# Emitting the steps of three recurrences behind every 24 products of a projection instead of every 12

## The chip, the cores and the metric

The kernel runs on one core of one Trainium2 chip. The metric is device time in microseconds (us); the kernel before took 1235.43 us, the median of three runs (1233.78 to 1237.32).

## What is computed

The reference is one layer of a hybrid model. 272 tokens (16 learned ones and 256 of the input, 2048 wide) are normalised and multiplied by one wide matrix. Its columns feed three mixers, each a recurrence over chunks of 64 tokens: A (`hgrn2`, 8 heads), B (`mlstm`, 4 heads) and C (`rwkv7`, 16 heads). Each result goes through a matrix and a gate, the three are added, and a last matrix and a norm follow:

```python
xn = rmsnorm(h, norm_g[l])
(a_q, a_f, ..., c_z, g_a, g_b, g_c) = split_cols(xn @ w_in[l])
y_a = hgrn2_mixer(a_q, a_f, a_i, a_z, ...)
y_b = mlstm_mixer(b_q, b_k, b_v, b_o, b_ig, b_fg, b_z, ...)
y_c = rwkv7_mixer(c_r, c_k, c_v, c_wd, c_ad, c_z, ...)
merged = (jax.nn.sigmoid(g_a) * (y_a @ w_br[l, 0])
          + jax.nn.sigmoid(g_b) * (y_b @ w_br[l, 1])
          + jax.nn.sigmoid(g_c) * (y_c @ w_br[l, 2]))
h = h + merged @ w_out[l]
return rmsnorm(h, final_norm_g)[:, N_META:]
```

## The kernel before, in words

**Precision and products.** Every weight and every activation is split into a high and a low half (`fp32r`), and a product of the reference becomes three matmuls: high by high, low by high, high by low. `unit` (line 379) does this for four row tiles of a weight block and one column tile: 12 matmuls.

**The weight stream.** `Stream` (from line 334) keeps four raw weight blocks of 128x1024 in flight (`load`, line 345, a transfer on SyncE's queue) and up to three split ones. `cut` (line 353) makes the halves: ScalarE copies the high one (`wh`), VectorE subtracts it for the low one (`wl`). Both happen inside `ws.next`, once for each block.

**The projections.** `gemm` (line 392) computes 256 columns for all tokens, transposed: four weight blocks, and in each of them two column tiles (`nt` is 2 for each call) of 12 matmuls into two PSUM banks of the tag `gp`, of which there are four. After the last block the banks are emptied (`evac`). The list `blocks` orders the projections: three of C's first group, the gates of B, then groups `b 0`, `c 1`, `b 1`, `c 2`, `a 0`, `a 1`, `c 3`, `a 2`, `a 3` (line 1591). A C group after the first is four calls of `gemm` (R, K, V, Z), an A group four (F, Q, I, Z), a B group eight. After these come the products of the gates and branches (`rows_gemm`, line 1358) and of the last matrix.

**The recurrences** are generators: `c_scan` (line 508), `b_scan` (967) and `a_scan` (1140). Each `yield` ends a step; `yield "pe"` says that the next step begins with a matmul. A C recurrence makes scores (`SC` from `RA` and `BK`), sends them through DRAM to a layout with 40 small matrices, inverts these in 31 steps on VectorE (`LV`, `Ltmp`, line 657), sends the result back (`scv`, `sct`, `Vm`, `VT`, lines 669 to 683), and then runs five chunks in order (line 733), each a chain of products and copies. It ends with a norm, with the bonus `cBV` added, in `Y["C"]` (lines 788 to 810). `cBV` uses the buffer of `cK`, which the next group's K projection writes.

**Who emits a step, and when.** `Order` (line 44) keeps a modelled clock for TensorE, ScalarE and VectorE while the program is written out. `pump` (line 87) goes through the open recurrences and emits steps as long as a step's modelled inputs are ready no later than 3.5 us after TensorE's clock; for a step that begins with a matmul the margin is 2.0 us for C and 0.3 us for A and B:

```python
ahead = self.AHEAD
if s["pe"]:
    ahead = self.AHEAD_PE if s["prio"] else self.AHEAD_PE_FIRST
if s["ready"] > self.clk["pe"] + ahead:
    break
self.step(s)
```

`finish` (line 105) emits all that is left of a recurrence. It is called where the next one needs its buffers: before C's next R projection (line 487), before the next head of B begins (950), before the next A recurrence begins (1124) and, up to the place where its tiles come free, before A's next F projection (1114). `pump` is called in `gemm` (line 399) and, after each three matmuls, in `rows_unit` (line 1356). The order in which the program is written out is a priority: the framework that builds it may place an instruction that it takes to be ready ahead of an earlier one that it takes to be waiting, unless `keep_in_program_order` is set (line 129).

Of the kernel before, what the change touches and what calls it, by code (L numbers as in the profile page):

```python
# [150 lines left out]
def kernel(  # L151
# [29 lines left out]
    od = Order()  # L181
# [197 lines left out]
    def unit(h, l, u, kts, ps, aH, aL, t0, n, js):  # L379
        for k in range(UK):  # L380
            kk = u * UK + k
            rh = aH[:, kk, t0:t0 + n]
            mm(ps, h[:, k, js], rh, start=kk == 0, stop=False)
            mm(ps, h[:, k, js], aL[:, kk, t0:t0 + n], start=False, stop=False)
            mm(ps, l[:, k, js], rh, start=False, stop=kk == kts - 1)

    def apart(f):
        saved, od.ready = od.ready, od.clk["pe"]
        f()
        od.ready = saved  # L390

    def gemm(m, aH, aL, kts, t0, n, evac):
        nt = m // P
        ps = [gps.tile([P, 512], F32, name="gp", tag="g") for _ in range(nt)]
        for u in range(kts // UK):
            h, l = ws.next()
            for j in range(nt):
                unit(h, l, u, kts, ps[j][:, 0:n], aH, aL, t0, n, slice(j * P, (j + 1) * P))
                od.pump()
        for j in range(nt):  # L400
            apart(lambda: evac(j, ps[j][:, 0:n]))

# [2 lines left out]
    def proj(c0, m, t0, evac, before=None, after=None):  # L405
        ws_src = win[:, :, c0:c0 + m]
        blocks.append((ws_src, KT, lambda: gemm(m, xH, xL, KT, t0, T - t0, evac), before, after))
# [1291 lines left out]
```

## Time and profile before

| what | before |
|---|---|
| median of 3 runs (lowest, highest) | 1235.43 us (1233.78, 1237.32) |
| the profiled execution's own time | 1238.05 us |
| its span, first to last instruction | 1236.3 us |
| TensorE matmuls busy | 1210.1 us |
| VectorE busy | 878.7 us |
| ScalarE busy | 665.7 us |

The profile is of one execution. PE is TensorE's matmul row, PEld its weight loads, DVE VectorE, ACT ScalarE, POOL GpSimd, and a q behind a name (SPq) is the engine's queue, which issues transfers. Times are counted from the first instruction. Matmuls are pipelined, so that a matmul shows as busy for some 0.28 us while the next starts 0.12 us after it. Nearly all instructions of VectorE and ScalarE carry line 127 and all matmuls line 186 (helpers), so tiles tell them apart: `gp` is a bank of a projection, `cbank` one of the C recurrence, `bank` one of A or B.

### The profile page before, as it was taken

To read this page: it belongs to the slowest core of one execution; us is meant where nothing else is said; L and a number is where in the kernel's file an instruction comes from. 1 tells how busy PE (TensorE), PEld (TensorE's weight loads), DVE (VectorE), ACT (ScalarE), POOL (GpSimd) and SP (SyncE) were. 2 spreads that over 40 slices of the span, in tenths; PEclk is the share of its full clock that TensorE was granted. 3 is DMA by queue.
4 is the path that set the end of the run, shared out by engine and by line. 5 is a ranking of instruction groups with operands and counts; after the bars stand their busy time and mean duration, and the time that the engine had idled before them with its cause. 6 is when DMAs were issued, how large, how long until landed. Compare 5 with 4: busy or idle time off the path is not lost.

```text
span 1236.3 us, 23074 instructions
## 1 busy us (share of the span) xinstructions
PE 1210.1 (98%) x9226; PEld 1106.3 (89%) x9226; DVE 878.7 (71%) x1489; ACT 665.7 (54%) x1032; POOL 57.2 (5%) x167
## 2 busy tenths in 40 slices
PE   7999999999999999999999999999999999999997
PEld 6999999999999999989999978888888888888887
DVE  5778897687985799995889986644555555556554
ACT  5764445564445764756764757544444444445444
POOL 3100000000041000000000000000000000000000
PEclk8999999999999999999999999999999999999999
DMA  8646555455563564554554454666766676665563
GB/s 211 186 142 175 159 156 137 137 168 157 157 178 103 154 163 139 154 154 116 150 169 130 139 164 135 205 189 191 231 191 193 198 219 198 196 190 171 193 196 120
DMA packets 173124, 207.43 MB, mean 168 GB/s; under 512 B 22395, under 2 KB 127224, under 8 KB 172632
## 3 DMA queue, kind: packets, MB, share of 16 engines
q1 hardware_dynamic: 172104, 202.73, 56.1%
q0 software_dynamic: 880, 3.22, 0.8%
q8 instruction: 72, 1.18, 0.4%
q14 instruction: 36, 0.29, 0.1%
q10 hardware_dynamic: 32, 0.01, 0.0%
HBM read 202.19 MB, written 3.74 MB: 167 GB/s over the span
## 4 chain that ended last, share of the span: by engine, by line
PE 84%; DVE 9%; ACT 3%; issue 2%; DMA 1%; SPq 0%; ACTq 0%; DVEq 0%
PE gp L186 76%; PE cbank L186 4%; DVE wl L127 3%; PE bank L186 3%; ACT wh L127 1%; DVE Ltmp L127 1%; DMA xt<-in_x_dram 1%; DVE LV L127 1%; PE cbank L193 1%; PE bank L193 1%; DVE UV L127 0%; DVE aM L127 0%; DVE aY L127 0%; ACT L127 0%; DVE aW L127 0%
## 5 line engine op out<-in xcount | busy, mean ns | idle before, releaser
L127 DVE TENSOR_TENSOR wl<-raw,wh 128x1024 fp32r<-128x1024 f32 (+1 forms) x370 | 449.1, 1215 | 242.2 <-ACT wh L127 240.7
L127 ACT CAST wh<-raw 128x1024 fp32r<-128x1024 f32 (+1 forms) x370 | 386.5, 1045 | 387.3 <-PE gp L186 358.2
L186 PE MATMUL gp<-xH,wh 128*128 128x272 f32 (+3 forms) x1552 | 449.5, 290 | 0.2 <-ACT xH L127 0.2
L186 PE MATMUL gp<-xH,wl 128*128 128x272 f32 (+3 forms) x1552 | 445.1, 287 | 1.6 <-DVE wl L127 1.6
L186 PE MATMUL gp<-xL,wh 128*128 128x272 f32 (+3 forms) x1552 | 444.8, 287 | 0.0
L186 PEld LDWEIGHTS gp<-xH,wl 128*128 128x128 f32 x1552 | 293.4, 189 | 3.0 <-DVE wl L127 2.7
L186 PEld LDWEIGHTS gp<-xH,wh 128*128 128x128 f32 x1552 | 293.7, 189 | 2.2 <-ACT xH L127 0.5
L186 PEld LDWEIGHTS gp<-xL,wh 128*128 128x128 f32 x1552 | 293.5, 189 | 0.8 <-DVE xL L127 0.2
L186 PE MATMUL gp<-wh,xH 128*128 128x512 f32 x384 | 150.7, 392 | 0.0
L186 PE MATMUL gp<-wh,xL 128*128 128x512 f32 x384 | 150.5, 392 | 0.0
L186 PE MATMUL gp<-wl,xH 128*128 128x512 f32 x384 | 150.2, 391 | 0.0
L186 PEld LDWEIGHTS gp<-wh,xL 128*128 128x128 f32 x384 | 72.1, 188 | 15.4
L186 PEld LDWEIGHTS gp<-wl,xH 128*128 128x128 f32 x384 | 72.2, 188 | 15.2
L186 PEld LDWEIGHTS gp<-wh,xH 128*128 128x128 f32 x384 | 72.1, 188 | 15.0
L186 PE MATMUL gp<-wh,mH 128*128 128x512 f32 (+1 forms) x144 | 51.1, 355 | 0.0
L186 PE MATMUL gp<-wl,mH 128*128 128x512 f32 (+1 forms) x144 | 51.0, 354 | 0.0
L186 PE MATMUL gp<-wh,mL 128*128 128x512 f32 (+1 forms) x144 | 50.9, 354 | 0.0
L127 DVE TENSOR_TENSOR LV<-LV,Ltmp 40x31 f32<-40x31 f32 (+15 forms) x124 | 41.0, 330 | 2.6
L127 DVE TENSOR_TENSOR Ltmp<-LU,LV 40x31 f32<-40x31 f32 (+15 forms) x124 | 41.0, 331 | 2.4
L186 PEld LDWEIGHTS gp<-wh,mL 128*128 128x128 f32 x144 | 27.2, 189 | 3.7
L186 PEld LDWEIGHTS gp<-wl,mH 128*128 128x128 f32 x144 | 27.2, 189 | 3.7
L186 PEld LDWEIGHTS gp<-wh,mH 128*128 128x128 f32 x144 | 27.2, 189 | 3.7
(412 smaller groups left out, 1476.5 us busy)
## 6 DMA issues: line engine op xcount, KB each, us to landing
raw<-in_w_in_dram SPq DMA_DIRECT2D x288, 512.0 KB, 3.6
raw<-in_w_br_dram SPq DMA_DIRECT2D x48, 512.0 KB, 3.8
raw<-in_w_out_dram SPq DMA_DIRECT2D x32, 512.0 KB, 3.6
hres<-in_x_dram POOLq DMA_DIRECT2D x2, 1024.0 KB, 5.8
raw<-in_w_in_dram SPq DMA_DIRECT2D x4, 256.0 KB, 2.9
fg<-in_final_norm_g_dram POOLq DMA_DIRECT2D x1, 1024.0 KB, 5.3
out_dram<-hres SPq DMA_DIRECT2D x4, 256.0 KB, 2.6
xt<-in_x_dram SPq DMA_DIRECT2D x3, 320.0 KB, 6.8
```

Source lines behind the costliest of these rows:

```text
L127: r = f(*a, **k)
L186: nc.tensor.matmul(o, lhsT, rhs, start=start, stop=stop)
L193: nc.tensor.transpose(o, a, i)
```

## The change

In `gemm` the call of `pump` moves out of the loop over the two column tiles. Steps of the recurrences are emitted after both tiles of a weight block, 24 matmuls, and no longer after each tile's 12.

```diff
@@ -396,7 +396,7 @@
             h, l = ws.next()
             for j in range(nt):
                 unit(h, l, u, kts, ps[j][:, 0:n], aH, aL, t0, n, slice(j * P, (j + 1) * P))
-                od.pump()
+            od.pump()
         for j in range(nt):
             apart(lambda: evac(j, ps[j][:, 0:n]))
```

## Rows read from the trace of the kernel before

**Rows 1.** The page: busy us (share of the span) xinstructions of each engine.

```profile
PE 1210.1 (98%) x9226; PEld 1106.3 (89%) x9226; DVE 878.7 (71%) x1489; ACT 665.7 (54%) x1032; POOL 57.2 (5%) x167
```

**Rows 2.** Busy time by stretch: length, each engine's busy us (xcount), clock, DMA.

```profile
core 0: us, PE busy (x) PEld busy (x) DVE busy (x) ACT busy (x) POOL busy (x), PEclk, DMA share, GB/s
40.00:771.00 731.00, 721.07 (x6891) 694.44 (x6891) 601.29 (x1177) 432.99 (x746) 45.09 (x131) 1.00 0.53 150
325.00:375.00 50.00, 50.00 (x457) 49.18 (x457) 42.88 (x85) 24.30 (x41) 16.22 (x62) 1.00 0.58 161
475.00:527.00 52.00, 50.42 (x577) 49.09 (x575) 50.44 (x117) 33.01 (x57) 0.32 (x2) 1.00 0.46 133
695.00:740.00 45.00, 41.97 (x537) 37.66 (x536) 40.81 (x93) 29.68 (x50) 1.01 (x2) 1.00 0.51 147
771.00:1128.00 357.00, 357.00 (x1574) 294.48 (x1573) 192.37 (x187) 160.02 (x170) 1.07 (x2) 1.00 0.66 200
```

**Rows 3.** Waits of TensorE's matmuls: for whom, us in total, times, longest us.

```profile
PE gp L186 <- DVE wl L127: 1.6, 4, 0.7
PE bank L186 <- DVE aW L127: 1.6, 2, 1.0
...
PE cbank L186 <- DVE SC L127: 1.5, 4, 0.6
PE cbank L186 <- issue: 1.4, 1, 1.4
PE bank L186 <- DVE aYL L127: 1.2, 2, 0.8
PE cbank L186 <- ACT cX L127: 0.9, 3, 0.3
```

**Rows 4.** Chain of waits, pumped stretch of 105 to 200 us: start, us, what.

```profile
128.48 1.41 PE gp L186 x12
...
130.33 4.26 PE gp L186 x36
...
141.14 5.64 PE gp L186 x48
...
154.56 10.69 PE gp L186 x84
```

**Rows 5.** Chain of waits, main loop of the first C recurrence.

```profile
217.96 1.70 PE gp L186 x12
...
219.76 0.68 PE cbank L186 x4
220.44 0.75 PE gp L186 x6
221.19 0.63 PE cbank L186 x4
...
222.64 0.85 PE cbank L186 x24
```

**Rows 6.** Instructions by shape, the two halves: busy us, mean ns, idle before.

```profile
L127 DVE TENSOR_TENSOR wl<-raw,wh 128x1024 fp32r<-128x1024 f32 x366 | 446.4, 1221 | 242.2 <-ACT wh L127 240.7
L127 ACT CAST wh<-raw 128x1024 fp32r<-128x1024 f32 x366 | 384.1, 1050 | 387.3 <-PE gp L186 358.2 <-issue 22.4 <-ACT osq L127 1.6
```

**Rows 7.** Timeline, end of the second C recurrence: start, us, instruction [idle before].

```profile
415.36 0.69 DVE L127 TENSOR_TENSOR cYc<-cYc,cBV 128x512 f32<-128x512 f32 x1
...
416.08 0.87 ACT L127 ACTIVATE cK<-gp,omu 128x272 f32<-128x272 f32 x2 [0.53 <-DVE cYc L127]
...
416.51 0.39 PE L186 MATMUL gp<-xH,wh 128*128 128x256 f32 x1
```

**Rows 8.** Timeline of SyncE's queue, second C recurrence.

```profile
356.28 0.39 SPq L669 DMA_DIRECT2D scv<-LV  x1
359.44 0.38 SPq L350 DMA_DIRECT2D raw<-in_w_in_dram  x1
359.87 0.42 SPq L197 DMA_DIRECT2D sct<-LT  x1
```

## The prediction

> **What bounds the kernel now.** I began with the page's engine totals [rows 1]: TensorE is busy 1210.1 us of the 1236.3 us span, VectorE 878.7. The table by stage came next [rows 2]. In it the reader should subtract the busy column of PE from the length of each stretch. Over the 731 us in which recurrences run, 9.9 us are left over; in the 357 us of gate and branch products none. Where the A and C recurrences crowd VectorE (50.44 of 52 us, 40.81 of 45 us) TensorE loses 1.58 and 3.03 us. Its granted clock is 1.00, the upper level of 2.4 GHz, in every row. So the projections bound the kernel, and the recurrences cost time only where a product of theirs, or a late weight half, makes TensorE wait.
>
> Then I asked who ends those waits [rows 3]. From 40 us on they are: the low weight half 1.6 us, `aW` 1.6, `SC` 1.5, one product 1.4 (listed as issue), `aYL` 1.2, `cX` 0.9; the rest are below 0.6 each. This list is the whole store that a different grain could empty.
>
> Last I read the chain of waits for how recurrence products sit among projection products. In a pumped stretch [rows 4] runs of `gp` products are 12, 36, 48 or 84 long: 12 last 1.41 us, and a run that is an odd multiple of 12 shows groups standing in the middle of a weight block. From 44 to 771 us I counted about 42 such mid-block positions in this view against some 30 at block ends. In the main loop of a C recurrence [rows 5] the runs are 6 and 12 and the groups come every 1.43 to 1.45 us: this part is emitted by `finish` when the next group opens (line 487), and the build then places each product by its own idea of readiness. That half of the work never sees the removed call.
>
> **The change, part by part.** No instruction is added or removed. Of about 376 pump calls in `gemm` every second one goes (47 calls of `gemm`, 4 blocks, 2 tiles); the pumps in `rows_unit`, every 3 products, stay.
>
> *What the steps are moved past.* Between the two pump places of a block the program emits 12 matmuls and nothing else. Loads are issued and halves cut only in `ws.next`, evacuations only after the last block. So on VectorE, ScalarE, GpSimd and SyncE a step moved from mid-block to block end passes nothing: its order against the split (1.05 us on ScalarE, 1.22 us on VectorE, [rows 6]) and against the weight load is the old one. Only on TensorE is it moved, behind 12 products: 1.41 us. Cost of the non-TensorE steps: 0. What covers it is that the test `ready <= pe + 3.5` at the block's end admits what the two tests admitted together; were that cover gone, a split would stand behind other steps than now, and its 1.22 us on VectorE could come late once in a block.
>
> *Products that were early.* A product placed 1.41 us later finds its input there. Both `aYL` waits (longest 0.8 us) are shorter than 1.41, and by my count of products from the start of the group both stand mid-block. I take 1.2 us off. The `aW` and `SC` waits stand partly at block ends or in steps forced by `finish`: bounds 0 and 3.1 us off; I take 0, since `SC` waits for a PSUM bank that VectorE empties just as late. The `aW` inputs hang on the same crowded VectorE.
>
> *Products that were just in time.* A chain of recurrence steps that passes through TensorE slips 1.41 us, or a whole block of 2.82 when it misses the next test. The tightest consumer I found is the handover after the second C group [rows 7]: `cYc` waits for the bonus `cBV` until 416.05, `cK` is evacuated at 416.08 (0.53 us idle for it), and the next projection's first product runs at 416.51. There is no slack. ScalarE and VectorE are in order there, so a late `cYc` holds both evacuations and, behind them, the bank that the product needs. I price it at one slip: +1.4 us. Bounds: 0, since two more banks may come free first, and 2.82.
>
> *A and B.* Their products have a margin of only 0.3 us and so slip by 1.41 or 2.82 us at a step rather than clump. Their results are needed by the branch products, hundreds of us later, and the first tile that the next head overwrites is one projection away (8 x 1.41 = 11.3 us). Cost 0; without that slack, 2.82 for the one head.
>
> *A step that slips a whole block* does pass one split and one load. For the transfers of a C recurrence that matters on SyncE [rows 8]: `scv` went at 356.28, then a weight load held the queue, and `sct` followed at 359.87, 3.2 us after `scv` had been issued (356.28 + 0.39). A slip past one more load is bounded by 0 and 3.2 us; I take 0, as the old program already has a load in that place.
>
> *Sum.* -1.2 + 1.4 = +0.2 us. The profiled execution took 1238.05 us (span 1236.3 and 1.75 around it), 2.62 above the median of the three runs, 1235.43. Made against the profile the sum gives 1238.25; carried to the median, **1235.6 us**.
>
> **A rule against the change.** The rows show TensorE filling the links of a dependent chain with projection products: 6 of them, 0.75 us, between two groups 1.43 us apart [rows 5]. In the Trainium skill, "TensorE: Matmul & The Clock Gate", section "Step-by-step: what each phase is for", matmuls stay in program order and only weight loads are pulled ahead. By that rule two dependent groups put at the same block end, if the build leaves them adjacent, would leave the 0.75 us of such a link open; the row agrees in so far as the six products there do stand between the groups. This gives the second rival its mechanism; the row gives its price.
>
> **The rivals.** The first ends on the other side: **the C chain comes late**. Place: the handover of [rows 7] and its like after the first group. Three `RA,BK` groups and two transposes of `cV` precede the triangular inverse, and each may miss a test. Price: 2 handovers x 2.82 = 5.6 us, so 1241.0; with one transfer held behind a load, 3.2 more, 1244.2. It decides once the end of a C recurrence moves by more than the slack, which is nil after the second group. For it: VectorE is 42.88 of 50 us busy while the second inverse runs [rows 2], so little is made up. Against: the main loop is emitted by `finish` at a fixed place, which a small slip doesn't move, and the evacuation of `cV` doesn't need the recurrence.
>
> **Clumps**: two dependent groups at one block end. I found five pairs 12 to 15 products apart inside one block (four `RA,BK`, one of the decay products). Price: 5 x 0.75 = 3.8 us, 1239.2. For it: `SC` is already a wait. Against: in [rows 5] the build itself put 6 products between such groups.
>
> **Waits dissolve**: every pumped wait goes (`aYL` 1.2, `SC` 1.5, `aW` 1.6) and no chain is late: -4.3, so 1231.1. For it: 42 groups get 1.41 us more for their inputs. Against: `aW` and `SC` follow VectorE, which stays as full.
>
> **It does not do what it says**: the build orders products by readiness, as [rows 5] shows, and the new program order yields nearly the old stream. 1235.4.
>
> **How the numbers follow.** Differences under 0.3% (3.7 us) can't be told from no change here: the three runs spread over 1233.78 to 1237.32. My forecast has 0.45, the unchanged stream 0.10, both within 0.3%; the late C chain 0.15, clumps 0.10, both slower; dissolved waits 0.20, faster. That makes 0.20, 0.55, 0.25. Low end: 1231.1 less half the spread of the runs, 1.8, or 1229.3. High end: the late chain with a held transfer, 1244.2. The middle of all four rivals is inside; I leave two in ten for what I have not thought of.
>
> **What would show it.** Right: the same instruction counts; runs of `gp` products in pumped stretches that are multiples of 24; no TensorE wait for `aYL`; VectorE order around the splits as before; idle TensorE between 40 and 771 us still about 9.9 us. Late chain: the product after the second C group's handover starts after a gap, with `cK` evacuated later against it than now, and `LV` ending later. Clumps: more wait on `SC` and `cX`, and fewer `gp` products between groups. Dissolved: `aW` and `SC` leave the list. Wrong altogether: the low weight half rises in the list of waits, because then VectorE's order did change, or the C main loop is no longer emitted by `finish`.

## The result, and the profile after

The changed kernel takes 1248.28 us in the median of four runs (1246.7 to 1250.05), the kernel before 1234.71 (four runs, 1233.78 to 1237.32): a ratio of 1.0109, 95% interval 1.009 to 1.0128. It is slower by some 13.6 us. That lies outside the range I gave, on the side of the first rival, and in a place that I had not named.

The profiled run of the changed kernel took 1246.7 us (span 1245.0). First its page: TensorE's total, and of the slices the rows of TensorE, of its clock and of what the transfers moved.

```profile
PE 1212.8 (97%) x9226; PEld 1108.1 (89%) x9226; DVE 874.6 (70%) x1489; ACT 664.4 (53%) x1032; POOL 54.8 (4%) x167
...
PE   8999999999999999999999996999999999999997
...
PEclk8999999999999999999999997999999999999999
...
GB/s 216 195 128 195 151 154 151 119 170 149 167 174 114 153 173 143 128 189 110 148 174 130 154 162 28 214 187 189 231 189 195 192 212 211 191 195 174 189 198 120
```

The work is the same as in [rows 1]: 9226 matmuls, 1489 VectorE instructions. The reader should look for the one slice that stands out. It is the 25th (747 to 778 us): TensorE busy six tenths, its clock seven tenths of full, and 28 GB/s where its neighbours move 162 and 214. Something stopped the stream of weights for a whole slice.

The stretches of [rows 2], as far as they matter here, and below them a cut that [rows 2] did not make, at 700 us. Columns: length, each engine's busy us, granted clock, DMA share, GB/s.

```profile
40.00:771.00 731.00, 712.75 (x6839) 686.47 (x6838) 591.91 (x1171) 424.26 (x734) 42.32 (x130) 0.99 0.53 149
695.00:740.00 45.00, 42.49 (x443) 37.06 (x443) 43.82 (x97) 21.90 (x33) 0.00 (x0) 1.00 0.60 173
771.00:1128.00 357.00, 356.42 (x1562) 294.17 (x1563) 192.97 (x189) 160.02 (x172) 1.64 (x3) 1.00 0.66 197
```

```profile
40.00:700.00 660.00, 653.03 (x6182) 1.00 0.54 151
700.00:800.00 100.00, 88.14 (x780) 0.93 0.47 139
```

The same cut of the kernel before:

```profile
40.00:700.00 660.00, 653.10 (x6163) 1.00 0.54 151
700.00:800.00 100.00, 96.97 (x855) 1.00 0.53 159
```

This cut is the whole reading. Up to 700 us TensorE is idle 6.97 us after and 6.90 before: over nine tenths of the stretch with recurrences, and nearly all the waits I had weighed, come to no difference. From 700 to 800 us it is idle 11.86 us against 3.03. That is 8.8 us, and the clock of 0.93 comes on top.

TensorE's waits, over the whole profile (for whom, us in total, times, longest us), against [rows 3]:

```profile
PE cbank L186 <- ACT UV L127: 3.8, 6, 1.2
PE gp L186 <- DVE wl L127: 3.6, 4, 1.4
PE bank L193 <- ACT xt L127: 3.2, 1, 3.2
PE cbank L186 <- ACT cX L127: 3.2, 6, 0.7
PE cbank L186 <- DVE cSL L127: 2.9, 1, 2.9
PE bank L186 <- DVE aQ L127: 1.8, 2, 1.1
...
PE cbank L186 <- DVE UV L127: 1.4, 1, 1.4
PE cbank L186 <- DVE SC L127: 0.4, 1, 0.4
```

`aYL` has left the list, `SC` fell from 1.5 to 0.4 us, `aW` from 1.6 to 0.2: what the rival of dissolving waits said did happen. In their place stand `UV`, `cX` and `cSL`. `UV` and `cX` are links of a C recurrence's main loop, between whose groups six projection products stood in [rows 5]; `cSL` belongs to the norm behind the loop.

Which products ran there? The next view is that of the tile `gp`, the projections' accumulator, in the stretch 742 to 774 us of the changed kernel (duration ns min/median/max, first and last start):

```profile
L186 PE MATMUL gp<-wh,xL x1: 396/396/396, 743.1 to 743.1; 128*128 128x512 f32 x1
...
L186 PE MATMUL gp<-wh,yHB x2: 628/628/628, 772.6 to 773.4; 128*128 128x512 f32 x2
```

The last product of the first gate block (the first 96 products behind the projections) starts at 743.1 us, and the next projection product of any kind at 772.6: 29.5 us without one. The longest such stretch in the kernel before, from 700 us on, is 3.6 us. What TensorE did meanwhile, by stretches:

```profile
743.00:755.00 12.00, 10.25 (x114) 1.00 0.33 92
755.00:763.00 8.00, 4.51 (x62) 0.86 0.00 0
763.00:772.00 9.00, 3.78 (x26) 0.50 0.00 0
772.00:775.00 3.00, 3.00 (x11) 0.59 0.03 5
775.00:790.00 15.00, 15.00 (x67) 1.00 0.62 194
```

Left alone with the dependent steps of the fourth C recurrence, and for a while of an A recurrence, it is less and less busy, and no weights are loaded since none are used. The products that end the hole multiply `yHB`. Their casts, and the evacuation `sg` of the gate block that was finished at 743, come on ScalarE only when the recurrence writes its last chunk `cY`:

```profile
768.73 0.19 ACT L127 COPY cY<-cbank 128x32 f32<-128x32 f32 x1 [1.14 <-PE cbank L186]
768.95 0.60 ACT L127 ACTIVATE sg<-gp 128x512 f32<-128x512 f32 x1
...
771.09 1.12 ACT L127 CAST yHB<-yB 128x512 fp32r<-128x512 f32 x2
```

In the kernel's text `l_setup` (lines 1342 to 1345) lets the fourth C recurrence finish, closes its pool and opens the pool that holds `sg`, `yHB` and the merged sums. Whether these two wait for the memory or for their place in ScalarE's queue no run here tells apart.

Why then was the recurrence late? Two lines of the tiles `RA` and `BK`, 600 to 660 us, of the kernel before:

```profile
L186 PE MATMUL cbank<-RA,BK x40: 272/272/373, 633.6 to 640.7; 64*128 64x128 f32 x32, 64*128 64x32 f32 x8
...
L127 DVE TENSOR_TENSOR BK<-cK,cE x4: 178/432/690, 625.1 to 626.5; 64x512 f32<-64x512 f32 x2, 64x32 f32<-64x32 f32 x2
```

and of the changed one:

```profile
L186 PE MATMUL cbank<-RA,BK x40: 272/272/373, 646.4 to 655.0; 64*128 64x128 f32 x32, 64*128 64x32 f32 x8
...
L127 DVE TENSOR_TENSOR BK<-cK,cE x4: 176/424/689, 630.7 to 633.0; 64x512 f32<-64x512 f32 x2, 64x32 f32<-64x32 f32 x2
```

The first row's start, 633.6 and 646.4, moved by 12.8 us. The last operation on the data it multiplies starts at 626.5 and 633.0: the product came 7 us after its input before, and 13 us after it now. In the changed kernel `RA` was complete at 621.9 us, and TensorE has no idle time before the product (its busy time, clock, DMA share and GB/s):

```profile
633.00:646.30 13.30, 13.30 (x110) 1.00 0.60 164
```

So it was not waiting for data; it stood later in the order of TensorE's instructions. The main loop, whose first products are `cbank<-VT,SC`, then starts at 739.6 us instead of 723.6.

### The profile page after: what moved, and what is told of

It is laid out like the page before. It is cut to its first block, busy times and chain, and to the rows that moved or that the text cites. A ratio compares the mean times of both kernels' runs of the same rounds, so it can differ in the third digit from the quotient of the medians.

```text
span 1245.0 us, 23073 instructions
## 1 busy us (share of the span) xinstructions
PE 1212.8 (97%) x9226; PEld 1108.1 (89%) x9226; DVE 874.6 (70%) x1489; ACT 664.4 (53%) x1032; POOL 54.8 (4%) x167
## 4 chain that ended last, share of the span: by engine, by line
PE 86%; DVE 9%; ACT 3%; issue 1%; DMA 1%; SPq 0%; ACTq 0%; DVEq 0%
PE gp L186 77%; PE cbank L186 5%; PE bank L186 2%; DVE wl L127 2%; ACT wh L127 1%; DVE LV L127 1%; DVE Ltmp L127 1%; PE cbank L193 1%; DMA xt<-in_x_dram 1%; PE bank L193 1%; DVE aM L127 0%; DVE aW L127 0%; DVE aY L127 0%; DVE UV L127 0%; DVE aRS L127 0%
```

## The experiments

Two theories are told apart. **Late end**: a test of the planner lets out about one step of the C recurrence, so half the tests make it slow; only the fourth one is paid for, because the projections that can cover its end run out. **Spread**: the coarser grain makes steps wait for one another, a little in every block. The planner is plain arithmetic in the kernel, so one can count how many of the fourth recurrence's 94 steps are out when the group is flushed: 71 before, 55 after. The expectations use that count.

**1 and 2. Which part of the run.** A flag `od.fine` chooses the grain; `mark` is the first block of the fourth C group.

```diff
-                od.pump()
+                if j == nt - 1 or od.fine:
+                    od.pump()
...
+    for nb, (src, kts, run, before, after) in enumerate(blocks):
+        od.fine = nb >= mark
```

> Edit: tests behind whole blocks of 24 up to the projections of the fourth C group, behind each 12 from there on. Theory (late end): the 13.6 us are lost only because the fourth C recurrence, whose steps the planner admits about one per test, ends later, and the projections that could run beside its end have run out; the three earlier ones were 5 to 9 us late for nothing. With fine tests for the fourth the time comes back to 1235 to 1241 us (the planner has 64 of its 94 steps out when the group is flushed, against 71 in the kernel before and 55 in the changed one, so some of it may stay). Rival (lateness is handed on from group to group): 1246 to 1248 us. Rival (clumps, a loss at every block): the blocks from there on are about a third, so 1243 to 1245 us.

Measured: 1239.29 us, ratio 1.0044 (1.0029 to 1.0059). The second kernel has `nb < mark`:

> Edit: the reverse; tests behind each 12 products up to the projections of the fourth C group, behind whole blocks from there on. Theory (late end): most of the loss is here, 1242 to 1248 us (62 of 94 steps out at the flush). Rival (handed on): about 1235 us. Rival (clumps at every block): a third of 13.6 us, 1238 to 1240 us.

Measured: 1241.28 us, ratio 1.0061 (1.0046 to 1.0076). The first falls in the late end's range, the second 0.7 us below it. "Handed on" expected about 1247 and 1235 and is out, and the shares of a loss at every block, 1243 to 1245 and 1238 to 1240, are missed on either side. The main loop starts at 729.2 and 731.8 us, the stretch without projection products is 10.6 and 15.4 us. But the two losses, 5.6 and 7.5 us, are closer to each other than I thought: how the planner stands when the fourth group begins matters as well as what it does in it.

**3. The hole by itself.** The changed kernel, with the second gate block emitted before the first block of the branch product; the recurrences are not touched.

```diff
         for jb in range(D // WB):
             one(jb)
+        if first:
+            blocks.insert(n0 + 1, blocks.pop(n0 + 2))
```

> Edit: the changed kernel, with the second gate block of branch B emitted ahead of the first block of its output product, so that 96 more products of 512 columns that need nothing of the recurrences stand behind the first 96. The recurrences come as late as in the changed kernel. Theory (late end: TensorE stands idle because nothing independent is left from 743 to 772 us): these 96 products, some 20 us, run in the hole, and 8 to 13 of the 13.6 us come back: 1235 to 1240 us. Rival (the loss is spread, by clumps or by lateness in the stretch before): nothing comes back, 1247 to 1249 us.

Measured: 1232.28 us, ratio 0.9989 (0.9979 to 0.9998). All of the loss is gone, more than the 8 to 13 us expected. Its trace has the recurrence as late as in the changed kernel (`VT,SC` at 739.1 us) and the hole filled. Busy time by stretch, and what TensorE did from 752 us:

```profile
40.00:700.00 660.00, 652.94 (x6182) 1.00 0.51 151
700.00:800.00 100.00, 98.14 (x839) 1.00 0.53 167
```

```profile
752.32 0.68 PE L186 MATMUL cbank<-UV,SC 128*128 128x128 f32 x4
752.76 0.47 PE L186 MATMUL gp<-wh,xH 128*128 128x512 f32 x1
...
753.99 0.57 PE L186 MATMUL cbank<-cX,Vm 128*128 128x64 f32 x4
754.37 0.47 PE L186 MATMUL gp<-wh,xL 128*128 128x512 f32 x1
```

Idle time from 700 to 800 us is 1.86 us where the changed kernel had 11.86, and between `UV,SC` and `cX,Vm` stand gate products again. This is the run that decides: with the same tests at the same places, the grain costs nothing once there is something to run. Spread expected 1247 to 1249.

**4. Emission or data.** Tests at block ends, but each admits more.

```diff
-    AHEAD = 3.5
-    AHEAD_PE = 0.3
-    AHEAD_PE_FIRST = 2.0
-    CAP = 5.0
+    AHEAD = 4.9
+    AHEAD_PE = 1.7
+    AHEAD_PE_FIRST = 3.4
+    CAP = 6.4
```

> Edit: tests behind whole blocks as in the changed kernel, but the planner's three margins and its cap are 1.4 us larger (4.9, 1.7, 3.4 and 6.4 us), half a block of its own clock, so that a test admits the next step as well. Theory (late end, by one step per test): the fourth recurrence is as far at the flush as in the kernel before (75 of 94 steps against 71), 1233 to 1238 us. Rival (clumps: steps that stand 24 products apart wait for each other, whatever the margin): stays at 1246 to 1249 us, or above, as larger margins issue steps before their inputs are there.

Measured: 1236.46 us, ratio 1.0026 (1.0016 to 1.0037), within the late end's 1233 to 1238. `RA,BK` and `VT,SC` of the fourth recurrence start at 626.7 and 714.8 us, earlier than in the kernel before. The steps still stand 24 products apart, so their spacing was not the cost; when they were let out was. What is left, 2.7 us, has its place partly before 700 us, where TensorE is busy 1.2 us less (651.92 of 660).

**5. Place or number.** One test a block, behind its first 12 products.

```diff
-                od.pump()
+                if j == 0:
+                    od.pump()
```

> Edit: one test for each block of 24, as in the changed kernel, but behind its first 12 products instead of behind all 24. Theory (it is the number of tests that paces the fourth recurrence): 57 steps out at the flush against the changed kernel's 55, so 1244 to 1248 us. Rival (it is the place: behind a whole block the steps stand next to the next block's split, or wait 12 products longer than they need): 1234 to 1238 us.

Measured: 1247.44 us, ratio 1.011 (1.0096 to 1.0123); `VT,SC` at 738.3 us, 28.1 us without projection products. The place within the block is worth nothing: the number of tests is.

**6 and 7. Whose steps.** The mid-block test admits one kind of recurrence only (`pump` gets a filter for its scans).

```diff
-                od.pump()
+                od.pump() if j == nt - 1 else od.pump(lambda s: not s["prio"])
```

> Edit: the test at mid block admits steps of the C recurrence alone; A's and B's are admitted behind whole blocks. Theory (late end of the fourth C recurrence): C's own steps have both tests again, but A's, which share VectorE's modelled clock with them, come in larger doses; the planner has 65 steps of the fourth recurrence out at the flush (71 before, 55 changed), so 1236 to 1241 us. Rival (A's and B's coarser steps cost the time): 1246 to 1249 us. Rival (only the number of tests counts, whatever they admit): 1233 to 1235 us.

Measured: 1245.07 us, ratio 1.009 (1.0074 to 1.0106), a miss by 4 us and near the rival that blames A's and B's grain. With `s["prio"]` in place of `not s["prio"]`:

> Edit: the reverse; the test at mid block admits A's and B's steps alone, C's behind whole blocks. Theory (late end of the fourth C recurrence): the planner has 58 of its steps out at the flush, near the changed kernel's 55, so 1243 to 1248 us. Rival (A's and B's coarser steps cost the time): 1233 to 1237 us.

Measured: 1241.69 us, ratio 1.0061 (1.0047 to 1.0075), a miss by 1.3 us on the other side, and far above that rival's 1233 to 1237. So restoring the tests for C alone gives back little, and for A and B alone about half. In the planner both charge one modelled VectorE clock, so neither's steps come out independently of the other's. In the traces the fourth main loop starts at 737.6 and 734.0 us, late in both, in the order of the times; my count of steps at the flush (65 and 58) had them the wrong way round. In run 7 the fourth inverse starts 2.3 us earlier than in the kernel before (first `LV` update at 647.3 against 649.6 us) and its last update comes 11.9 us later (720.6 against 708.7): C's own 31 steps had half the tests. In run 6 it starts 7.3 us later and its last update comes 14.6 us later, though C had all its tests; what holds it up there is not shown. With C alone there is a second cost, busy 650.50 of 660 us before 700, and in TensorE's waits of that kernel (40 to 800 us) the low weight half has risen from 1.6 to 5.6 us:

```profile
PE gp L186 <- DVE wl L127: 5.6, 7, 1.6
```

**8. The hole in the kernel before.** The edit of run 3 on the fine tests.

> Edit: the kernel before (a test behind each 12 products), with the second gate block of branch B emitted ahead of the first block of its output product. Theory: in the kernel before, the products beside the end of the fourth recurrence last almost to its end, so little is left to fill: TensorE is idle 3.0 us between 700 and 785 us, and the change can give back that at most: 1230 to 1234 us. If it is no faster than the changed kernel with the same edit (1232.3 us), then with the hole filled the fineness of the tests costs and saves nothing that can be measured; the rival, that coarse tests also cost something in the stretch before, expects it 2 us or more below that one.

Measured: 1233.74 us, ratio 1.0002 (0.9993 to 1.0011): nothing to fill, nothing gained. Coarse with the hole filled (1232.28) is not slower than fine with it filled, which leaves nothing for a spread loss.

**9 and 10. Finer still.** In `unit`, a test after 6 of the 12 products as well; run 10 adds the two gate blocks.

```diff
             mm(ps, l[:, k, js], rh, start=False, stop=kk == kts - 1)
+            if k % 2 == 1 and k < UK - 1:
+                od.pump()
```

> Edit: the kernel before with four times the tests of the changed one, behind each 6 products (the order of the blocks as before). Theory (the number of tests paces the fourth recurrence, and only the hole at its end costs): the fourth recurrence ends some us earlier than in the kernel before, but there TensorE had only 3.0 us of idle time between 700 and 785 us, so 1231 to 1234 us. Rival (each finer dose is worth as much as the last): 24 to 12 products gave 13.6 us, 12 to 6 would give 5 to 7 us, 1227 to 1229 us. Rival (steps issued before their inputs are there, and TensorE waits for them in order): 1236 to 1242 us.

Measured: 1241.87 us, ratio 1.0065 (1.0042 to 1.0087).

> Edit: tests behind each 6 products and the second gate block of branch B emitted ahead of the first block of its output product. Theory: with the hole filled the fineness of the tests is worth nothing, so the time is that of the coarse kernel with two gate blocks (1232.3 us) within 2 us. Rival (fine tests also save waits before 700 us): 1228 to 1230 us.

Measured: 1243.93 us, ratio 1.0068 (1.005 to 1.0087). Both miss the theory and the expectation of a steady gain; the third reading, steps let out too early, has the size. There is no hole (3.1 us at most in either). The loss is before 700 us, as the stretches of run 9 show, and so the extra gate block can't help:

```profile
40.00:700.00 660.00, 649.97 (x6123) 1.00 0.54 150
700.00:800.00 100.00, 97.78 (x872) 1.00 0.54 161
```

Its waits name the low weight half and `SC`, against 1.6 and 1.5 us in [rows 3]:

```profile
PE gp L186 <- DVE wl L127: 4.1, 4, 1.4
PE cbank L186 <- DVE SC L127: 3.6, 5, 1.3
```

That is 4.6 us of the 7.8. Nor is the fourth recurrence earlier than at 12 products (`VT,SC` at 727.7 and 731.6 us against 723.6). The rest goes with TensorE's clock. Three of run 9's six executions had a mean granted clock of 0.996 and took 1237.7 to 1240.3 us; the other three, at 0.991 or 0.986, took 1243.4 to 1248.5. In run 10 two at 0.996 took 1238.3 and 1239.4 us, and four at 0.990 or 0.991 took 1243.5 to 1245.5. So at the higher clock the finer tests cost 3.6 to 6.2 us, and the 2 us between the two medians say nothing of the gate block; where the clock fell is shown at the end. So of these grains 12 products are best: at 6 weights and steps wait on VectorE, at 24 the last recurrence is late.

**11. Both cures at once**: the margins of run 4 and the gate blocks of run 3.

> Edit: the changed kernel with margins larger by 1.4 us and with the two gate blocks. Theory: the margins alone left 2.7 us over the kernel before although the fourth recurrence came 9 us earlier than there; that is put down to steps issued too early (1.2 us less TensorE work done from 40 to 700 us), which the gate blocks don't cure: 1233 to 1237 us. Rival (what is left there is the end of the recurrences too): 1230 to 1232 us.

Measured: 1236.53 us, ratio 1.002 (1.0011 to 1.0029). As expected: with the recurrence early there is no hole, and the 2.4 us that the margins cost stay.

**12. Run 3 again.**

> Edit: none against the run with the changed kernel and two gate blocks; it is taken again beside the others. Theory: 1231.5 to 1233 us, 0.1% below the kernel before, an interval that just leaves out 1. If it comes out within 0.05% of the kernel before, then no version here beats that one measurably.

Measured: 1233.75 us, ratio 0.9995 (0.9986 to 1.0003). The interval of the first run left out 1, this one does not, so the kernel with coarse tests and two gate blocks is as fast as the kernel before; that it is faster is not established.

The kernels side by side. "Bare" is the longest stretch from 700 us on, start to start, without a projection product; times in us. The medians of the kernel before that were taken beside the experiments are 1233.73 (1 to 4), 1233.75 (5 to 8) and 1234.1 (9 to 12).

| kernel | `VT,SC` of the fourth | bare | TensorE idle 40 to 700 | idle 700 to 800 | median |
|---|---|---|---|---|---|
| before | 723.6 | 3.6 | 6.9 | 3.0 | 1234.7 |
| changed | 739.6 | 29.5 | 7.0 | 11.9 | 1248.3 |
| 1, fine from the fourth group | 729.2 | 10.6 | 7.2 | 6.2 | 1239.3 |
| 2, coarse from the fourth group | 731.8 | 15.4 | 6.9 | 5.7 | 1241.3 |
| 3, changed, two gate blocks | 739.1 | 3.5 | 7.1 | 1.9 | 1232.3 |
| 4, larger margins | 714.8 | 3.3 | 8.1 | 1.6 | 1236.5 |
| 5, test at mid block only | 738.3 | 28.1 | 6.1 | 12.0 | 1247.4 |
| 6, C at mid block | 737.6 | 10.2 | 9.5 | 6.2 | 1245.1 |
| 7, A and B at mid block | 734.0 | 12.1 | 7.2 | 5.7 | 1241.7 |
| 8, before, two gate blocks | 720.9 | 2.8 | 7.0 | 1.6 | 1233.7 |
| 9, a test each 6 | 727.7 | 3.1 | 10.0 | 2.2 | 1241.9 |
| 10, a test each 6, two gate blocks | 731.6 | 3.1 | 9.9 | 2.2 | 1243.9 |
| 11, larger margins, two gate blocks | 714.6 | 3.3 | 8.0 | 1.6 | 1236.5 |
| 12, as 3 | 741.2 | 3.5 | 7.1 | 1.8 | 1233.8 |

## Why the prediction was wrong

**The step that failed** is the cover under the non-TensorE steps: "the test `ready <= pe + 3.5` at the block's end admits what the two tests admitted together". It does not. After a test the steps of A and the weight splits have charged the planner's VectorE clock up to the margin or past it, so the next step of C is priced to end beyond `pe + 3.5`, and the loop mostly stops after that one step. The planner's arithmetic for the fourth recurrence, carried through for both kernels (its own clock, us; steps counted from 0):

```
                 before                          changed
step   issued at pe   its end          issued at pe   its end
 13        700.7       705.4               739.8       743.8
 14        702.1       706.2               742.4       746.4
 15        703.4       708.2               745.2       749.1
 16        704.7       709.2               748.0       751.6
 23        715.7       720.7               763.2       768.1
```

In the changed column step 14 ends at 746.4 while the test stands at 742.4: 746.4 > 742.4 + 3.5, so the test ends there, and step 15 waits for the next one, 2.8 us on. In the column before, step 14 ends at 706.2 > 702.1 + 3.5 and the test ends as well, but the next is 1.3 us on. About one step per test in both, with half the tests: steps 13 to 23 take 15.0 us before and 23.4 after. I had treated the test as a gate on readiness, when on a crowded VectorE it is a metronome. The runs that show it: more margin at the same tests (run 4) brings the recurrence back, another place for as many tests (run 5) does not. The prediction had priced the loss of this cover at a split's 1.22 us, late once in a block; the waits for the low weight half rose by only 2.0 us in all (1.6 to 3.6), and the loss came at the end of the fourth recurrence instead, as 29.5 us without projection products and 8.8 us more idle time.

**The other points, in their order.**

- *Waits.* I took 1.2 us off for `aYL` and nothing for `aW` and `SC`; all three fell, by 1.2, 1.4 and 1.1 us. Others rose as much, and 40 to 700 us came out even (6.90 and 6.97 us idle).
- *The handover after the second C group* [rows 7], +1.4 us: it did not happen. From 405 to 425 us TensorE is busy 20.00 of 20.00 us, and so it was in the kernel before. I had read "no slack" from instructions that follow closely on one another; the rows show the bonus being added to `cYc` until 416.05, not a wait for it, and TensorE idle nowhere. The second recurrence ended only 0.4 us later than before although its `RA,BK` products were 7.6 us late. The first and the third ended 5.1 and 7.2 us later, and nothing waited for them (the expectation of run 1 puts all three at 5 to 9 us, which the second does not bear out).
- *A and B, cost 0.* Their results were in time, but their grain is not free: with it coarse alone (run 6) the kernel takes 11.3 us more than the one before. That this goes through the planner's VectorE clock, which A and B share with C, fits its arithmetic but was not tested by itself.
- *The order on VectorE*, which I had said would stand, changed. A step late by a block does pass a split, and most steps here were late by blocks: between the last `BK` operation (633.0 us) and `cRL` (640.1 us), VectorE does three splits and eight operations of A; in the kernel before (626.5 to 632.0 us) it was two and four.
- *The range* reached to 1244.2 us, the late C chain priced at two handovers and a held transfer. The mechanism of that rival was right and its place was wrong: I looked for the handover from one C group to the next, where other work covers it, and not for the last one, behind which `l_setup` puts the gate and branch products. That handover has no next projection: 96 products, and then nothing. My argument against the rival, that `finish` fixes the main loop's place, held for the program's text; but a `finish` that has 39 steps to emit rather than 23 leaves more of them behind the last covered product. The chances of the forecast and its four rivals also added up to 1, so they left nothing for what I had not thought of.
- *What would show me wrong* did: the last update of `LV` in the fourth recurrence started at 726.1 us instead of 708.7, the low weight half rose to 3.6 us, and idle TensorE between 40 and 771 us is 18.25 us, not 9.9.

**The sum as it was.** Between the two profiled executions the time differs by 8.65 us (1246.7 and 1238.05). The one of before had started 2.6 us late, in its wait for the first tile of x (`xt`: 5.8 us in its list of waits, 3.2 in the list above), so 11.3 us were lost after that. 8.8 us of them are TensorE's idle time between 700 and 800 us, 0.1 that before 700. The remaining 2.4 us I did not trace one by one; the lowered clock below lies in that stretch, and TensorE's busy total rose by 2.7 us (1210.1 to 1212.8) for the same 9226 matmuls.

## What to carry to other kernels

When a scheduler emits about one step per test, the number of tests paces a dependent chain, unless wider margins let more steps out (run 4); ask how many steps a test really lets out on a loaded engine before you call one redundant. More tests are not always better: at 6 products the chain was no earlier and TensorE waited more. A late chain is free as long as independent work stands behind it, so price it at the last place where that work runs out, and look there first: moving one independent block ahead of a dependent one was worth the whole 13.6 us here. And a count of idle time by stretch, cut where the recurrences end, shows this at once, where a sum over the run hides it.

## What the runs showed of the hardware

I had not expected the clock to fall. In the changed kernel TensorE's granted clock went from 1.00 to 0.50, the lower level of 1.2 GHz, at about 761 us, after a stretch in which TensorE was never idle for more than 1.2 us at a time but was less and less busy (10.25 of the 12 us from 743 to 755, 3.02 of the 6 us from 755 to 761). It came back at about 774 us, after the first four projection products. In between the same groups of the main loop take longer:

```profile
760.95 0.69 PE L186 MATMUL cbank<-UV,BT 128*64 128x64 f32 x8 [1.19 <-ACT UV L127]
...
763.88 1.19 PE L186 MATMUL cbank<-UV,SC 128*128 128x128 f32 x4 [1.38 <-DVE UV L127]
...
772.57 0.63 PE L186 MATMUL gp<-wh,yHB 128*128 128x512 f32 x1
...
774.81 0.39 PE L186 MATMUL gp<-wh,yLB 128*128 128x512 f32 x1
```

`UV,SC` takes 1.19 us here and 0.68 us with the hole filled (run 3, where the clock stays at 1.00); a projection product 0.63 us and then 0.39. The Trainium skill, "TensorE: Matmul & The Clock Gate", section "What's actually happening", gives the same two levels and says that activity is what releases the lower one. The trace agrees in so far as the level rose once projection products ran again.

From 700 to 800 us every kernel whose bare stretch is at most 3.6 us shows 1.00, and the six with a longer one show 0.91 to 0.98. But a bare stretch is not needed. In run 10 the clock fell to 0.50 after a single wait of 1.25 us (for `SC`, until 635.5 us) and stayed there for about 10 us, in which TensorE was busy throughout (length, busy time, clock, DMA share, GB/s):

```profile
632.00:636.00 4.00, 2.75 (x28) 1.00 0.54 151
636.00:640.00 4.00, 4.00 (x26) 0.68 0.51 141
640.00:644.00 4.00, 4.00 (x17) 0.50 0.15 24
644.00:648.00 4.00, 4.00 (x21) 0.54 0.60 179
```

In run 9, whose tests are the same and whose blocks differ only further on, TensorE waited 1.24 us at the same place and all these rows show 1.00. The fourth main loop then started at 727.7 us, in run 10 at 731.6: this is what some 10 us at the lower level cost. In runs 5, 6 and 7 the clock fell for about 3 us between 670 and 681 us, after waits of 1.61, 1.62 and 2.36 us for the low weight half. Why one wait is followed by a fall and another is not, no run here shows.
